# Two rounded token halves on ScalarE, the exact ones on VectorE, and the norm ahead in VectorE's queue

## The chip, the cores and the metric

The kernel runs on one core of a Trainium2 chip. The time is that of one execution on the device, in microseconds. The core's engines are TensorE (PE in the rows: matrix products and transposes; PEld is its weight load), VectorE (DVE), ScalarE (ACT), GpSimd (POOL) and SyncE (SP, which here only issues loads). They run side by side, each through its own queue, in the queue's order, and wait for each other through semaphores.

## The reference

Two layers of a decoder trunk on one sequence of 256 tokens with 1024 features, all in float32. Cut to what matters here:

```python
for l in range(2):
    mod = silu(c) @ w_ada[l] + b_ada[l]
    sh_m, sc_m, gt_m, sh_f, sc_f, gt_f = split(mod, 6)
    h = rms_norm(x, g_pre_mix[l]) * (1 + sc_m) + sh_m
    y = token_mixer(h, ...)                    # projection, two kinds of attention, output projection
    x = x + gt_m * rms_norm(y, g_post_mix[l])
    h = rms_norm(x, g_pre_ffn[l]) * (1 + sc_f) + sh_f
    y = conv_glu_ffn(h, ...)                   # (gelu(conv(h @ w_up_act)) * (h @ w_up_lin)) @ w_down
    x = x + gt_f * rms_norm(y, g_post_ffn[l])
```

The place of the change is the pair of lines between two sub-layers: the residual with its norm, and then the next sub-layer's norm and modulation.

## The kernel before

**Split numbers.** A product of full precision is made of three products of rounded numbers. Each operand is divided into a high part, rounded to the format fp32r (`hh` for tokens, `wh` or `dh` for weights), and a low part, the exact value less the high part (`hl`, `wl`, `dl`). `mm3` (L567 to L569) and `project` (L391) add high x high, low x high and high x low. A weight's split (`split`, L139 and L140) is a rounding copy on ScalarE and a subtraction on VectorE, each over 128x1024.

**Token tiles.** The 256 tokens are two tiles of 128. `xt` holds the running tokens with token rows on partitions. The products need the transposed form, with features on partitions: `hh` and `hl` have eight feature blocks of 128 (k = 0 to 7) by 256 tokens.

**A boundary.** `boundary` joins two sub-layers. There are three: mixer to FFN in layer 0, FFN of layer 0 to mixer of layer 1, and mixer to FFN in layer 1. Its inputs `ys` are four PSUM banks with the sub-layer's output, two halves of 512 features for each token tile. For each tile:

- `residual`: ScalarE squares each half with a running sum (L254), VectorE multiplies it by the gate row (L318, the gated product), GpSimd makes the factor one over the root (L262, L264), and VectorE adds the scaled product to `xt` (L326, two halves).
- `stat`: ScalarE squares the new tokens (L254), and GpSimd makes the second factor.
- `norm_T`: VectorE multiplies by this factor (L286, two halves), and TensorE transposes the halves, four 128x128 blocks (L274) into one PSUM bank each.
- `mod_T`: each block is multiplied by a column `scale` and gets a column `bias`. The rounded first half (k = 0 to 3) is written by ScalarE straight from the bank, block by block (L297). The second half is made exactly by VectorE (L300, four blocks, to an SBUF tile) and rounded by a copy on ScalarE (L305). The exact first half is made once more by ScalarE (L307, four blocks). At the end VectorE subtracts rounded from exact to get the low halves (L309, two of them).

**Order.** The program is traced in Python order; a compile-time scheduler then puts each engine's instructions into a queue, by the order of tracing and by when it reckons their inputs ready. `tc.issue_after(ins)` ties what is traced in its block, on the engine of `ins`, to a place behind `ins`. In a boundary the residual of tile 1 runs as a generator: its steps are taken between those of tile 0, and its last step (L326) is tied behind tile 0's last L300.

**After a boundary** to the FFN the first products are those of `lin`, 512 columns of `w_up_lin`, whose four weight units are loaded and split ahead, before the last rows of the output projection; the last unit (k = 6 and 7) takes its output buffer from the pool that the output projection's weights use. For each token tile `project` first runs all products with `hh`, and only then those with `hl` (`late="h"`). After the boundary to the mixer come the index projections `ia` and `ib`, with rotary embedding on VectorE (L357, L362), transposes (L368), index scores (L434) and the choice of the 64 best keys (L445, L446). Between them run products of the modulation on VectorE (L189).

Of the kernel before, what the change touches and what calls it, by code (L numbers as in the profile page):

```python
# [13 lines left out]
AF = mybir.ActivationFunctionType  # L14
OP = mybir.AluOpType
# [59 lines left out]
def trunk(ctx: ExitStack, tc, plan, x, c, stream, small, rope, out):  # L75
    nc = tc.nc
# [10 lines left out]
    def bank(i):  # L87
        return ps.tile([128, 512], F32, name=f"b{i}", tag=f"b{i}")
# [7 lines left out]
    def t2(dt=F32):  # L96
        return wrk.tile([128, 512], dt, name="t2", tag="t2", bufs=12)

    def big(name, dt=F32):
        return wrk.tile([128, 4, S], dt, name=name, tag="big", bufs=6)  # L100

    def tiny(n):
        return wrk.tile([128, n], F32, name=f"tiny{n}", tag=f"tiny{n}", bufs=8)


    st = {"off": 0, "behind": ()}

    def load(*units):

        n = sum(u[3] for u in units)  # L110
        t = wts.tile([128, 2048], F32, name="raw", tag="raw", bufs=6)
        nc.sync.dma_start(t[:, :n], bass.AP(tensor=stream.tensor, offset=stream.offset + st["off"],
                                            ap=[[n, 128], [1, n]]))
        st["off"] += 128 * n
        plan.append(units)
        r, o = [], 0
        for u in units:
            r.append(t[:, o:o + u[3]])
            o += u[3]
        return r  # L120

    def split(raw, where=None, pin=False, gain=None):
        n = raw.shape[-1]
        if where is None:
            hi = wts.tile([128, 1024], F32R, name="wh", tag="wh", bufs=5)
            lo = wts.tile([128, 1024], F32R, name="wl", tag="wl", bufs=5)
        else:
            hi = big("dh", F32R).rearrange("p a b -> p (a b)")
            lo = big("dl", F32R).rearrange("p a b -> p (a b)")
        with ExitStack() as behind:  # L130
            for ins in st["behind"]:
                behind.enter_context(tc.issue_after(ins))
            put = tc.keep_in_program_order if pin else lambda ins: ins
            if gain is not None:
                put(nc.scalar.activation(out=hi[:, :n], in_=raw, func=AF.Copy, scale=gain))
                put(nc.vector.scalar_tensor_tensor(out=lo[:, :n], in0=raw, scalar=gain, in1=hi[:, :n].bitcast(F32),
                                                   op0=OP.mult, op1=OP.subtract))
                return hi, lo
            put(nc.scalar.activation(out=hi[:, :n], in_=raw, func=AF.Copy))  # L139
            put(nc.vector.tensor_tensor(out=lo[:, :n], in0=raw, in1=hi[:, :n].bitcast(F32), op=OP.subtract))  # L140
        return hi, lo


    xt = con.tile([128, 2, D], F32, name="xt")
# [107 lines left out]
    def square(src, n, s, to=None):  # L252

        nc.scalar.activation(out=t2(BF) if to is None else to, in_=src, func=AF.Square, scale=float(n) ** -0.5, accum_out=s)  # L254

    def inv_root(s):

        r = tiny(1)
        if s.shape[-1] == 1:
            nc.gpsimd.tensor_scalar(out=r, in0=s, scalar1=EPS, scalar2=None, op0=OP.add)  # L260
        else:
            nc.gpsimd.tensor_scalar(out=r, in0=s[:, 0:1], scalar1=s[:, 1:2], scalar2=EPS, op0=OP.add, op1=OP.add)  # L262
        r2 = tiny(1)
        nc.gpsimd.tensor_tensor(out=r2, in0=r, in1=mhalf, op=OP.pow)  # L264
        return r2
# [5 lines left out]
    def turn4(x, b):  # L271
        p = bank(b)
        for j in range(4):
            nc.tensor.transpose(p[:, 128 * j:128 * j + 128], x[:, 128 * j:128 * j + 128], ident)  # L274
        return p

    def stat(t):
        s = tiny(2)
        for h in range(2):
            square(xt[:, t, 512 * h:512 * h + 512], D, s[:, h:h + 1])  # L280
        return inv_root(s)

    def norm_T(t, r, banks):
        xn = [t2(), t2()]
        for h in range(2):
            nc.vector.tensor_scalar(out=xn[h], in0=xt[:, t, 512 * h:512 * h + 512], scalar1=r, scalar2=None,  # L286
                                    op0=OP.mult)
        return [turn4(xn[h], banks[h]) for h in range(2)]

    def mod_T(p, t, scale, bias, hh, hl, between=None):  # L290

        part = lambda h, j: dict(scale=scale[:, 4 * h + j:4 * h + j + 1], bias=bias[:, 4 * h + j:4 * h + j + 1])
        quarter = lambda y, j: y[:, 128 * j:128 * j + 128]
        place = lambda y, h: y[:, 4 * h:4 * h + 4, 128 * t:128 * t + 128]
        f = t2(), t2()
        for j in range(4):
            nc.scalar.activation(out=place(hh, 0)[:, j], in_=quarter(p[0], j), func=AF.Identity, **part(0, j))  # L297
        for j in range(4):
            m = part(1, j)
            d = nc.vector.tensor_scalar(out=quarter(f[1], j), in0=quarter(p[1], j), scalar1=m["scale"],  # L300
                                        scalar2=m["bias"], op0=OP.mult, op1=OP.add)
        if between:
            between(d.ins)
        wide = [x.rearrange("p (k t) -> p k t", k=4) for x in f]
        nc.scalar.activation(out=place(hh, 1), in_=wide[1], func=AF.Copy)  # L305
        for j in range(4):
            a = nc.scalar.activation(out=quarter(f[0], j), in_=quarter(p[0], j), func=AF.Identity, **part(0, j))  # L307
        for h in (0, 1):
            d = nc.vector.tensor_tensor(out=place(hl, h), in0=wide[h], in1=place(hh, h).bitcast(F32), op=OP.subtract)  # L309
        return a.ins, d.ins  # L310

    def residual(t, y, g, to=None):

        s = tiny(2)
        d = [t2(), t2()]
        for h in range(2):
            square(y[h], D, s[:, h:h + 1])
            nc.vector.tensor_tensor(out=d[h], in0=y[h], in1=g[:, 512 * h:512 * h + 512], op=OP.mult)  # L318
            if h == 0:
                yield  # L320
        r = inv_root(s)
        yield
        parts = [(0, 512), (512, 256), (768, 256)] if to is not None and t else [(0, 512), (512, 512)]
        for i, (o, n) in enumerate(parts):
            xo = xt[:, t, o:o + n]
            nc.vector.scalar_tensor_tensor(out=xo, in0=d[o // 512][:, o % 512:o % 512 + n], scalar=r, in1=xo,  # L326
                                           op0=OP.mult, op1=OP.add)
            if to is not None:
                (nc.scalar if i % 2 else nc.sync).dma_start(to[:, o:o + n], xo)
        yield  # L330

    def boundary(ys, g, scale, bias, hh, hl):

        r0, r1 = residual(0, ys[0], g), residual(1, ys[1], g)
        for _ in range(3):
            next(r0)
        s0 = stat(0)
        next(r1)
        p0 = norm_T(0, s0, (4, 5))
        next(r1)  # L340

        def second(ins):
            with tc.issue_after(ins):
                next(r1)

        a = mod_T(p0, 0, scale, bias, hh, hl, second)
        s1 = stat(1)
        p1 = norm_T(1, s1, (6, 4))
        return a, mod_T(p1, 1, scale, bias, hh, hl)
# [23 lines left out]
    def project_units(l, name):  # L373
        n = len(CCOLS[name])
        per = 1024 // n
        u = [("b" if name == "lin" else "w", l, (name, k, min(per, 8 - k)), min(per, 8 - k) * n) for k in range(0, 8, per)]
        return [u[i:i + 2] for i in range(0, len(u), 2)]
# [383 lines left out]
    hh, hl, opened, first = start()  # L761

    for l in range(DEPTH):
# [90 lines left out]
        ys = [[bank(0), bank(1)], [bank(2), bank(3)]]  # L854
# [27 lines left out]
        while st["out"] < 2:  # L882
# [1 line left out]
        bg.run(out_first(range(3)))  # L884
        bg.drain("att", "out")
        out_load(4, 8)
        first = [[split(raw, "lin" if g < 1 or u < 1 else None) for u, raw in enumerate(load(*us))]
                 for g, us in enumerate(project_units(l, "lin"))]
        raws = []
        bg.run(out_last(range(3, 8)))  # L890
        bg.drain("sf")
# [2 lines left out]
        hh, hl = hT_tiles()  # L894
        scale, bias = pre_scale(l, "ffn")
        gate = gates["mix"]
        st["behind"] = boundary(ys, gate, scale, bias, hh, hl)[1]


        w0, w1, w2, bc = (scol(l, n) for n in ("w0", "w1", "w2", "bc"))  # L900
        ys = [[bank(0), bank(1)], [bank(2), bank(3)]]
        pend = []
        lin = [wrk.tile([128, 512], F32, name="lin", tag="o", bufs=3).rearrange("p (j t) -> p j t", j=2)
               for _ in range(2)]
# [68 lines left out]
        gate = gates["ffn"]  # L973
        bg.run(down(pend, (0, 1)))
        tps["free"] = [6, 7]
        if l + 1 < DEPTH:
            hh, hl = hT_tiles()
            scale, bias = pre_scale(l + 1, "mix")
# [85 lines left out]
```

## Time and profile before

| what | value |
|---|---|
| median of 3 runs | 690.02 us (689.62 to 690.02) |
| profiled execution | 689.88 us |
| its span in the trace | 688.1 us |
| TensorE busy | 664.8 us, 97% |
| VectorE busy | 547.6 us, 80% |
| ScalarE busy | 424.8 us, 62% |
| GpSimd busy | 26.2 us, 4% |

The span is what the profiler records of one execution; the 1.78 us between it and the execution's own time lie around it. A busy TensorE is not one at its peak, since products are pipelined. Times in the rows are microseconds from the start of the span; the granted clock of TensorE is at its full level in all stretches that the rows show.

### The profile page before, as it was taken

To read this page: it belongs to the slowest core of one execution; us is meant where nothing else is said; L and a number is where in the kernel's file an instruction comes from. 1 tells how busy PE (TensorE), PEld (TensorE's weight loads), DVE (VectorE), ACT (ScalarE), POOL (GpSimd) and SP (SyncE) were. 2 spreads that over 40 slices of the span, in tenths; PEclk is the share of its full clock that TensorE was granted. 3 is DMA by queue.
4 is the path that set the end of the run, shared out by engine and by line. 5 is a ranking of instruction groups with operands and counts; after the bars stand their busy time and mean duration, and the time that the engine had idled before them with its cause. 6 is when DMAs were issued, how large, how long until landed. Compare 5 with 4: busy or idle time off the path is not lost.

```text
span 688.1 us, 11317 instructions
## 1 busy us (share of the span) xinstructions
PE 664.8 (97%) x4329; PEld 569.6 (83%) x4329; DVE 547.6 (80%) x1085; ACT 424.8 (62%) x787; POOL 26.2 (4%) x56
## 2 busy tenths in 40 slices
PE   7999898999999999999999999999999999999996
PEld 4887676777999999999988677777789999999994
DVE  5878999878899999897679985677689886666553
ACT  5556687886955555555576558878696555555441
POOL 1000000002000000000020000000200000000001
PEclk9999999999999999999999999999999999999999
DMA  8999558963499998987436642346246885655001
GB/s 362 419 415 372 181 203 332 370 219 123 183 332 379 379 361 340 340 328 281 168 140 245 275 133 114 123 168 220 103 172 232 320 316 183 217 184 184 1 1 61
DMA packets 24518, 163.04 MB, mean 237 GB/s; under 512 B 3312, under 2 KB 3728, under 8 KB 6160
## 3 DMA queue, kind: packets, MB, share of 16 engines
q1 hardware_dynamic: 23184, 159.77, 61.8%
q0 software_dynamic: 704, 2.11, 1.0%
q8 instruction: 34, 0.56, 0.3%
q10 hardware_dynamic: 576, 0.43, 0.2%
q14 instruction: 20, 0.16, 0.1%
HBM read 161.24 MB, written 1.06 MB: 236 GB/s over the span
## 4 chain that ended last, share of the span: by engine, by line
PE 76%; DVE 12%; ACT 6%; issue 3%; POOL 1%; DMA 1%; SPq 0%; POOLq 0%; DVEq 0%; ACTq 0%
PE b L569 18%; PE b L567 18%; PE b L568 18%; PE b L391 12%; PE b L726 3%; DVE wl L140 3%; PE b L411 2%; DVE iscore L434 2%; ACT t L479 1%; DVE iscore L446 1%; ACT t L254 1%; DVE tiny L445 1%; PE b L494 1%; DVE raw L684 1%; DMA raw<-in_stream_dram 1%
## 5 line engine op out<-in xcount | busy, mean ns | idle before, releaser
L140 DVE TENSOR_TENSOR wl<-raw,wh 128x1024 fp32r<-128x1024 f32 (+1 forms) x146 | 172.8, 1195 | 36.9 <-ACT wh L139 31.3
L567 PE MATMUL b<-hh,wh 128*128 128x256 f32 x640 | 179.9, 281 | 0.0
L569 PE MATMUL b<-hl,wh 128*128 128x256 f32 x640 | 179.6, 281 | 0.0
L568 PE MATMUL b<-hh,wl 128*128 128x256 f32 x640 | 179.6, 281 | 0.0
L139 ACT ACTIVATE wh<-raw 128x1024 fp32r<-128x1024 f32 (+1 forms) x146 | 149.0, 1047 | 41.9 <-PE b L569 37.0
L568 PEld LDWEIGHTS b<-hh,wl 128*128 128x128 f32 x640 | 122.5, 191 | 1.3
L567 PEld LDWEIGHTS b<-hh,wh 128*128 128x128 f32 x640 | 120.2, 188 | 1.5
L569 PEld LDWEIGHTS b<-hl,wh 128*128 128x128 f32 x640 | 120.1, 188 | 0.0
L189 DVE SCALAR_TENSOR_TENSOR raw<-raw,crow 128x1024 f32<-128x1024 f32 x72 | 86.6, 1218 | 1.9 <-DMA raw<-in_stream_dram 1.9
L391 PE MATMUL b<-wh,hh 128*128 128x512 f32 (+1 forms) x184 | 73.0, 399 | 0.1
L391 PE MATMUL b<-wh,hl 128*128 128x512 f32 (+1 forms) x184 | 68.5, 387 | 0.0
L140 DVE TENSOR_TENSOR dl<-raw,dh 128x1024 fp32r<-128x1024 f32 (+2 forms) x47 | 56.8, 1211 | 13.2 <-ACT dh L139 12.4
L139 ACT ACTIVATE dh<-raw 128x1024 fp32r<-128x1024 f32 (+2 forms) x47 | 49.6, 1060 | 25.6 <-PE b L568 25.6
L944 ACT ACTIVATE t<-b,smt 128x256 f32<-128x256 f32 x44 | 25.1, 571 | 57.9 <-PE b L569 57.9
L567 PE MATMUL b<-dh,t 128*128 128x512 f32 x152 | 59.7, 393 | 0.0
L568 PE MATMUL b<-dh,t 128*128 128x512 f32 x152 | 59.6, 392 | 0.0
L569 PE MATMUL b<-dl,t 128*128 128x512 f32 x152 | 59.2, 389 | 0.0
L391 PE MATMUL b<-wl,hh 128*128 128x512 f32 (+1 forms) x184 | 55.6, 392 | 1.0 <-DVE wl L140 1.0
L391 PEld LDWEIGHTS b<-wh,hh 128*128 128x128 f32 x184 | 34.7, 189 | 8.7 <-issue 1.7
L391 PEld LDWEIGHTS b<-wl,hh 128*128 128x128 f32 x184 | 33.8, 189 | 7.2 <-DVE wl L140 1.4
L391 PEld LDWEIGHTS b<-wh,hl 128*128 128x128 f32 x184 | 33.8, 188 | 6.2 <-issue 0.6
L945 DVE SCALAR_TENSOR_TENSOR t<-b,smt,t 128x255 f32<-128x255 f32 x44 | 21.1, 480 | 20.6 <-ACT t L944 20.4
(172 smaller groups left out, 1098.5 us busy)
## 6 DMA issues: line engine op xcount, KB each, us to landing
raw<-in_stream_dram SPq DMA_DIRECT2D x143, 1024.0 KB, 5.9
raw<-in_stream_dram SPq DMA_DIRECT2D x8, 804.0 KB, 9.6
gate<-gated POOLq DMA_DIRECT2D x4, 512.0 KB, 6.5
xt<-in_x_dram SPq DMA_DIRECT2D x2, 512.0 KB, 4.3
raw<-in_stream_dram SPq DMA_DIRECT2D x1, 984.0 KB, 5.1
out_dram<-xt SPq DMA_DIRECT2D x2, 256.0 KB, 2.1
raw<-in_stream_dram SPq DMA_DIRECT2D x1, 328.0 KB, 4.2
out_dram<-xt ACTq DMA_DIRECT2D x1, 256.0 KB, 2.1
```

Of the source, the lines that this page charges most:

```text
L139: put(nc.scalar.activation(out=hi[:, :n], in_=raw, func=AF.Copy))
L140: put(nc.vector.tensor_tensor(out=lo[:, :n], in0=raw, in1=hi[:, :n].bitcast(F32), op=OP.subtract))
L189: nc.vector.scalar_tensor_tensor(out=ri, in0=ri, scalar=1.0, in1=crow, op0=OP.mult, op1=OP.mult, accum_out=mods[l][:, j + i:j + i + 1])
L391: mm = lambda l_, k, i, start=False, stop=False: nc.tensor.matmul(a[:, :n], lhsT=l_[:, k, tt], rhs=w[k][i], start=start, stop=stop)
L411: ins = nc.tensor.matmul(out, lhsT=lhsT, rhs=rhs, **flags)
L434: nc.vector.scalar_tensor_tensor(out=sc, in0=r[:, j * nk:j * nk + nk], scalar=wi[:, h:h + 1], in1=fill[:, 256 - nk:] if first else sc, op0 ...
L567: nc.tensor.matmul(y, lhsT=hh, rhs=wh, start=first, stop=False)
L568: nc.tensor.matmul(y, lhsT=hl, rhs=wh, start=False, stop=False)
L569: nc.tensor.matmul(y, lhsT=hh, rhs=wl, start=False, stop=last)
L726: pin(nc.tensor.matmul(acc[n, t], lhsT=y[:, k, 128 * t:128 * t + 128], rhs=w[k, u][part][:, c:c + m],  start=k == 0 and y is hh and part = ...
L944: nc.scalar.activation(out=z, in_=p[:, :256], func=AF.Identity, scale=w2[:, i:i + 1], bias=bc[:, i:i + 1])
L945: nc.vector.scalar_tensor_tensor(out=z[:, 1:], in0=p[:, :255], scalar=w1[:, i:i + 1], in1=z[:, 1:], op0=OP.mult, op1=OP.add)
```

## The change

In `mod_T` VectorE now makes both exact halves from the PSUM banks, the second half first, and ScalarE makes both rounded halves block by block from the same banks; the rounding copy from SBUF and ScalarE's exact quarters go. In `boundary` the norm of tile 0 is traced ahead of the first step of tile 1's residual (a square and a gated product). In the two boundaries to the FFN, the split of the last `lin` unit is traced behind that norm, with its VectorE half tied behind the norm's second instruction. The number of loads and of products stays.

```diff
     def norm_T(t, r, banks):
...
-            nc.vector.tensor_scalar(out=xn[h], in0=xt[:, t, 512 * h:512 * h + 512], scalar1=r, scalar2=None,
-                                    op0=OP.mult)
-        return [turn4(xn[h], banks[h]) for h in range(2)]
+            d = nc.vector.tensor_scalar(out=xn[h], in0=xt[:, t, 512 * h:512 * h + 512], scalar1=r, scalar2=None,
+                                        op0=OP.mult)
+        return [turn4(xn[h], banks[h]) for h in range(2)] + [d.ins]
...
         for j in range(4):
             nc.scalar.activation(out=place(hh, 0)[:, j], in_=quarter(p[0], j), func=AF.Identity, **part(0, j))
+        for h in (1, 0):
+            for j in range(4):
+                m = part(h, j)
+                d = nc.vector.tensor_scalar(out=quarter(f[h], j), in0=quarter(p[h], j), scalar1=m["scale"],
+                                            scalar2=m["bias"], op0=OP.mult, op1=OP.add)
+            if h and between:
+                between(d.ins)
         for j in range(4):
-            m = part(1, j)
-            d = nc.vector.tensor_scalar(out=quarter(f[1], j), in0=quarter(p[1], j), scalar1=m["scale"],
-                                        scalar2=m["bias"], op0=OP.mult, op1=OP.add)
-        if between:
-            between(d.ins)
+            a = nc.scalar.activation(out=place(hh, 1)[:, j], in_=quarter(p[1], j), func=AF.Identity, **part(1, j))
         wide = [x.rearrange("p (k t) -> p k t", k=4) for x in f]
-        nc.scalar.activation(out=place(hh, 1), in_=wide[1], func=AF.Copy)
-        for j in range(4):
-            a = nc.scalar.activation(out=quarter(f[0], j), in_=quarter(p[0], j), func=AF.Identity, **part(0, j))
...
-    def boundary(ys, g, scale, bias, hh, hl):
+    def boundary(ys, g, scale, bias, hh, hl, extra=None):
...
         s0 = stat(0)
+        p0 = norm_T(0, s0, (4, 5))
+        if extra:
+            extra(p0[-1])
         next(r1)
-        p0 = norm_T(0, s0, (4, 5))
         next(r1)
...
-        first = [[split(raw, "lin" if g < 1 or u < 1 else None) for u, raw in enumerate(load(*us))]
-                 for g, us in enumerate(project_units(l, "lin"))]
+        first = [load(*us) for us in project_units(l, "lin")]
+        first[0] = [split(raw, "lin") for raw in first[0]]
+        first[1][0] = split(first[1][0], "lin")
+
+        def last_split(ins):
+
+            st["behind"] = (ins,)
+            first[1][1] = split(first[1][1])
+            st["behind"] = ()
+
...
-        st["behind"] = boundary(ys, gate, scale, bias, hh, hl)[1]
+        st["behind"] = boundary(ys, gate, scale, bias, hh, hl, last_split)[1]
```

## Rows read from the trace of the kernel before

**Rows 1.** The page, busy us of each engine (share of the span) x instructions

```profile
PE 664.8 (97%) x4329; PEld 569.6 (83%) x4329; DVE 547.6 (80%) x1085; ACT 424.8 (62%) x787; POOL 26.2 (4%) x56
```

**Rows 2.** Windows: from:to and length, busy us (x instructions) by engine

```profile
core 0: us, PE busy (x) PEld busy (x) DVE busy (x) ACT busy (x) POOL busy (x), PEclk, DMA share, GB/s
162.00:172.00 10.00, 8.63 (x43) 6.43 (x43) 7.77 (x18) 7.10 (x21) 1.72 (x4) 1.00 0.46 179
351.00:361.00 10.00, 9.03 (x63) 8.11 (x62) 9.06 (x18) 8.85 (x23) 1.75 (x4) 1.00 0.56 212
492.00:502.00 10.00, 9.06 (x45) 6.67 (x44) 7.58 (x17) 7.22 (x21) 1.72 (x4) 1.00 0.29 106
```

**Rows 3.** Timeline of TensorE, first boundary: start, us, what, [idle before, releaser]

```profile
162.58 1.09 PE L274 MATMUL b<-ident,t 128*128 128x128 f32 x8 [0.43 <-DVE t L286]
163.78 0.50 PE L391 MATMUL b<-dh,hh 128*128 128x512 f32 x1
...
166.40 0.50 PE L391 MATMUL b<-dh,hh 128*128 128x512 f32 x1 [0.49 <-ACT hh L305]
...
168.36 0.84 PE L391 MATMUL b<-dh,hl 128*128 128x512 f32 x3
169.54 1.11 PE L274 MATMUL b<-ident,t 128*128 128x128 f32 x8 [0.34 <-DVE t L286]
...
171.65 0.39 PE L391 MATMUL b<-dh,hh 128*128 128x512 f32 x1
```

**Rows 4.** Timeline of VectorE, first boundary

```profile
160.30 1.23 DVE L140 TENSOR_TENSOR wl<-raw,wh 128x1024 fp32r<-128x1024 f32 x1 [0.60 <-ACT wh L139]
...
162.05 0.88 DVE L286 TENSOR_SCALAR t<-xt,tiny 128x512 f32<-128x512 f32 x2
...
163.71 1.37 DVE L300 TENSOR_SCALAR t<-b,prescale,mod 128x128 f32<-128x128 f32 x4
164.99 1.41 DVE L326 SCALAR_TENSOR_TENSOR xt<-t,tiny,xt 128x512 f32<-128x512 f32 x2
166.73 1.29 DVE L309 TENSOR_TENSOR hl<-t,hh 128x512 fp32r<-128x512 f32 x2 [0.33 <-ACT t L307]
169.00 0.88 DVE L286 TENSOR_SCALAR t<-xt,tiny 128x512 f32<-128x512 f32 x2 [0.97 <-POOL tiny L264]
```

**Rows 5.** Timeline of ScalarE, first boundary

```profile
163.28 1.51 ACT L297 ACTIVATE hh<-b,mod,prescale 128x128 fp32r<-128x128 f32 x4 [0.40 <-PE b L274]
...
166.56 0.66 ACT L254 ACTIVATE t<-xt 128x512 bf16<-128x512 f32 x1
```

**Rows 6.** Timeline of GpSimd, first boundary

```profile
159.95 0.56 POOL L264 TENSOR_TENSOR tiny<-tiny,mhalf 128x1 f32<-128x1 f32 x1
...
168.40 0.56 POOL L264 TENSOR_TENSOR tiny<-tiny,mhalf 128x1 f32<-128x1 f32 x1
```

**Rows 7.** Waits of VectorE in the whole span: total us, times, longest

```profile
DVE t L318 <- ACT t L254: 15.1, 10, 2.7
```

**Rows 8.** Timelines of VectorE and of GpSimd, second boundary

```profile
349.36 0.69 DVE L318 TENSOR_TENSOR t<-b,gate 128x512 f32<-128x512 f32 x1 [1.37 <-ACT t L254]
...
354.48 1.41 DVE L326 SCALAR_TENSOR_TENSOR xt<-t,tiny,xt 128x512 f32<-128x512 f32 x2
...
358.03 0.88 DVE L286 TENSOR_SCALAR t<-xt,tiny 128x512 f32<-128x512 f32 x2 [0.94 <-POOL tiny L264]
...
349.23 0.56 POOL L264 TENSOR_TENSOR tiny<-tiny,mhalf 128x1 f32<-128x1 f32 x1
```

**Rows 9.** Timeline of VectorE, third boundary

```profile
495.07 1.40 DVE L326 SCALAR_TENSOR_TENSOR xt<-t,tiny,xt 128x512 f32<-128x512 f32 x2
...
498.77 0.88 DVE L286 TENSOR_SCALAR t<-xt,tiny 128x512 f32<-128x512 f32 x2 [0.97 <-POOL tiny L264]
```

**Rows 10.** Windows behind the second boundary, columns as in rows 2

```profile
358.10:378.60 20.50, 20.03 (x126) 17.78 (x127) 20.50 (x44) 13.79 (x30) 1.16 (x2) 1.00 0.60 216
378.60:379.70 1.10, 1.10 (x7) 0.89 (x6) 0.43 (x4) 1.10 (x3) 0.00 (x0) 1.00 1.00 283
```

**Rows 11.** Timeline of TensorE at the choice of keys, layer 1

```profile
402.12 0.63 PE L368 MATMUL b<-ident,t 128*128 128x128 f32 x4 [0.65 <-DVE t L362]
```

## The prediction

> **What bounds the kernel now.** I read the busy times first. TensorE is busy for 97% of the span [rows 1], so time can only be won where it waits. Next I read the three stretches in which one sub-layer ends and the next begins, called here the first, second and third boundary (from 162, 351 and 492 us). In each, TensorE leaves 0.9 to 1.4 us of 10 unused [rows 2]: 1.37 + 0.97 + 0.94 = 3.3 us in all, which is 0.5% of the time. That is about all that a change inside these stretches can give, and 0.2% (1.38 us) is about what a measurement of this kernel can tell from no change.
>
> Then I read the timelines of the first boundary, engine by engine. TensorE stands still at three places [rows 3]. The transposes of token tile 0 wait 0.43 us for the norm (L286). The fifth pair of products waits 0.49 us for the second half of the rounded tokens (L305). The transposes of tile 1 wait 0.34 us for the second norm. VectorE has waits of its own here, 0.33 us before the low halves (L309) and 0.97 us before the second norm [rows 4]. These two are the only room that it has for more work. They add up to 1.30 us.
>
> **The change, part by part.**
>
> *Norm first (first and third boundary).* The factor of tile 0 is ready on GpSimd at 159.95 + 0.56 = 160.51 [rows 6], but VectorE takes a weight split at 160.30, then the gated product of tile 1, and the norm only at 162.05 [rows 4]. After the change the norm starts at 160.55, and TensorE has its input before the output projection ends at about 162.15 (162.58 less the idle 0.43). The wait of 0.43 us goes. This does not make VectorE free earlier: split, norm and two gated products still have to run before the modulation (L300). Before, they and a short wait filled 160.30 to 163.71, 3.41 us [rows 4]. Started at 160.55 they end by 163.96 at the latest; without that wait they end near 163.76. I take 163.8, which is 0.1 later than before. The split's ScalarE half keeps its place, since its output buffer is freed by the projection in both versions, and its result is needed only for the last quarter of the first products, so its delay of about 1.2 us is hidden by the products before them.
>
> *Rounded tokens by quarters on ScalarE.* The copy of the second half (L305) goes, and four quarters, one per 0.35 us (1.51 us for four [rows 5]), take the place of the four quarters that made the exact first half (L307). ScalarE has the copy less to do per tile.
>
> The trace says what the new quarters wait for. VectorE's gated product (L318) needs nothing that ScalarE's square of the same bank (L254) makes, and yet it waited for that square ten times, 15.1 us in all [rows 7]. So two engines' reads of one bank follow each other in traced order, and the new quarters of the second half come behind all four of VectorE's quarters. The Trainium skill has this as a rule ("PSUM — Partial Sum Buffer", section on bank collisions): two engines may not touch one bank at once, reads included. The trace agrees, with the ten waits named. Without that order the quarters could start behind the first four, at 163.28 + 1.38 = 164.66, and the products would not stop at all; with it they start at 163.8 + 1.37 = 165.2.
>
> With 165.2, the first quarter reaches TensorE about 0.5 us later (as 163.28 led to 163.78 [rows 3, 5]), at 165.7 instead of 166.40. So TensorE comes 0.7 us earlier to the point where it wants the low halves: 167.66 instead of 168.36 [rows 3].
>
> *Exact first half on VectorE.* This is the term that eats the gain. Four quarters more per tile cost VectorE 1.3 us (L300 starts at 163.71 and L326 at 164.99 [rows 4]), twice per boundary. The residual of tile 1 (L326) is queued directly behind the second half's quarters, so the new quarters come behind it. From 163.8: L326 at 165.1, new quarters at 166.5 (L326 holds 1.41), low halves at 167.8, first one done at about 168.5, both at 169.1, then the second norm at 169.1. Before, low halves began at 166.73 and the norm at 169.00. TensorE, ready at 167.66, now waits for the low halves until 168.5; it came there at 168.36. The squares of tile 1 start at 165.2 + 1.38 = 166.6, as before (166.56 [rows 5]), so the second factor still comes at 168.40 + 0.56 [rows 6]. In short, VectorE's 1.30 us of room is filled with 1.3 us of work, and what TensorE won earlier it waits out here.
>
> *First boundary, sum.* From the first low-half product at 168.36 to the next tile's products at 171.65 TensorE has 3.29 us, 0.34 of them idle [rows 3], so 2.95 of work. Started at 168.5 it can end at 171.45: 0.2 us won. If the queue still puts three products ahead of the transposes, these wait for the norm as before and 0.1 is lost. I take -0.2, ends -0.4 and +0.1. In tile 1 nothing waited, and 1.3 us more on VectorE fit ahead of its first FFN split.
>
> *Second boundary.* No split is moved, and TensorE had work until its transposes anyway. VectorE: L326 at 354.48, so new quarters at 355.89, low halves at 357.19, both done at 358.48; the second norm began at 358.03 [rows 8]. It is 0.45 us later, and 0.9 if the first norm is also queued ahead of the gated product of tile 1: that began at 349.36, and the norm's factor came only at 349.23 + 0.56 = 349.79 [rows 8], so VectorE would stand idle for 0.43 first. TensorE can fill a little with the other projection: +0.3. What follows weighs more. From 358.1 to 378.6 VectorE is busy 20.50 of 20.50 us, and in the 1.10 us after it has 0.67 free [rows 10]. Behind that come the index scores and the choice of keys, in which TensorE waits for VectorE's rotary results, 0.65 us at 402.12 [rows 11]. The second boundary puts 0.45 + 1.3 = 1.75 us into this full stretch (1.3 for tile 1, with no idle time to take it); 0.67 is absorbed, and 1.1 reaches this wait. It can be less: the modulation products (L189) in this stretch are wanted only at the end of the mixer, and the compile-time order may let one of them, 1.2 us, slip behind. Ends for the second boundary: 0 and +1.5 (0.9 + 1.3 - 0.67). I take +0.9, nearer the upper one, since the stretch is full.
>
> *Third boundary.* L326 at 495.07, new quarters 496.48, low halves 497.78 to 499.07; the second norm began at 498.77 [rows 9]. It is 0.3 late; TensorE can use part of that for low-half products that it had left behind the transposes. I take +0.05, ends -0.2 and +0.3. The DMA queues see no new transfer; the buffer of the moved split comes free some 1.2 us later, which counts only if a load is late, and no wait for a load stands on TensorE here.
>
> *Sum.* -0.2 + 0.9 + 0.05 = +0.75 us; the lower ends give -0.6, the upper ends +1.9. The profiled execution took 689.88 us (span 688.10 and 1.78 around it), so 690.63. The median of the runs, 690.02, lies 0.14 above that execution, so I say 690.8.
>
> **Rivals.**
>
> *VectorE takes the new quarters in its waits (faster).* Its two waits of the first boundary equal the new work in length, 1.30 us. If the order put two of the new quarters into each, the low halves would not be late, and what the earlier rounded tokens win would stay: 0.7 + 0.2 from the second transposes in the first boundary, about 0.3 in the second, 0.5 in the third, with nothing carried on behind the second: -1.7 us, 688.3. Against it: the first wait, 0.33, holds one quarter, and the queue is in order. If the reads of one bank did not wait for each other, as above, 0.5 more per boundary would be open, but the low halves would hold TensorE all the same.
>
> *The full stretch carries it all (slower).* The place is VectorE from 349 to 402 us. The price: the first norm queued ahead of the ready product (0.9 in place of 0.45), 1.3 for tile 1, only 0.67 absorbed: +1.5 there, and +0.4 if the other two boundaries keep their old order on TensorE. That makes +1.9, 691.9. It decides once more than 1.4 us reaches the wait at 402.12. For it speaks the row with 20.50 of 20.50; against it that L189 can slip.
>
> *The change doesn't act where it is meant to.* In the second boundary the gated product is ready before the factor [rows 8] and can stay ahead; the quarters just change places between two engines. Then only the first boundary's 0.43 moves, and that is given back before the low halves: 690.0.
>
> **How the numbers follow.** The forecast, some tenths up to one us slower, has 0.52; no effect 0.12; the faster rival 0.13; the slower one 0.23. Only the last two go past 1.38 us, so faster 0.13, same 0.64, slower 0.23. The range from 688.9 to 692.1 holds the ends of the sum and both sides up to where one in ten is left out on each.
>
> **What would show it.** After the change, I expect in the first boundary transposes with no wait for L286, the second half's first quarter on ScalarE right behind VectorE's fourth, a new TensorE wait of 0.5 to 0.9 us for the low halves, and second transposes at about the old place. Behind the second boundary VectorE should stay full past 378.6, with the wait at 402 moved by about 1 us. The prediction is wrong if VectorE takes the new quarters before L326 or between the low halves without delay, if tile 1's norm comes earlier than before, or if the order of index scores and key choice changes on VectorE, which the trace of before can't show.

## The result, and the profile after

The changed kernel takes 698.34 us (median of 4 runs, 698.28 to 698.71) against 689.89 us before (4 runs). The ratio is 1.0119, 95% interval 1.0107 to 1.0132: 8.45 us, or 1.2%, slower, where +0.8 us was forecast and 692.1 was the upper end of the range. The profiled execution took 698.71 us with a span of 696.9 us.

The windows of the three boundaries after, at the places that answer to [rows 2] (the later two have moved by 4 and 6 us), and four short windows behind the first boundary's low halves. Columns as in [rows 2]; PEclk is the granted clock as a share of 2.4 GHz:

```profile
162.00:172.00 10.00, 7.78 (x37) 5.58 (x36) 8.14 (x19) 6.02 (x18) 2.53 (x4) 0.94 0.46 176
355.00:365.00 10.00, 7.86 (x54) 6.80 (x53) 9.15 (x19) 7.80 (x18) 3.04 (x4) 1.00 0.57 211
498.00:508.00 10.00, 7.92 (x40) 5.63 (x38) 8.36 (x20) 5.97 (x18) 2.52 (x4) 1.00 0.30 106
168.00:170.00 2.00, 0.74 (x2) 0.30 (x2) 1.16 (x4) 0.00 (x0) 1.43 (x2) 1.00 0.00 0
170.00:172.00 2.00, 1.91 (x10) 1.78 (x11) 0.98 (x4) 1.21 (x4) 0.00 (x0) 0.71 0.03 8
172.00:174.00 2.00, 2.00 (x6) 1.55 (x5) 2.00 (x7) 0.30 (x1) 0.00 (x0) 0.50 0.00 0
174.00:176.00 2.00, 2.00 (x9) 1.59 (x9) 0.78 (x2) 1.93 (x6) 0.00 (x0) 0.94 0.00 0
```

TensorE leaves 2.1 to 2.2 us of ten unused in each boundary, where it left 0.9 to 1.4 [rows 2]; GpSimd, column five, is busy 2.5 to 3.0 us instead of 1.7. And between 170 and 176 the clock is not at full speed all the time: in one window it is 0.50, the lower of the two levels (1.2 GHz).

TensorE's timeline in the first boundary after (answers to [rows 3]):

```profile
161.87 1.03 PE L274 MATMUL b<-ident,t 128*128 128x128 f32 x8
...
165.46 0.50 PE L393 MATMUL b<-dh,hh 128*128 128x512 f32 x1 [0.20 <-ACT hh L306]
...
168.76 0.74 PE L393 MATMUL b<-dh,hl 128*128 128x512 f32 x2 [1.18 <-DVE hl L309]
170.09 1.32 PE L274 MATMUL b<-ident,t 128*128 128x128 f32 x8 [0.59 <-DVE t L286]
171.06 2.06 PE L393 MATMUL b<-dh,hl 128*128 128x512 f32 x4
172.92 1.05 PE L393 MATMUL b<-wh,hl 128*128 128x512 f32 x2
173.77 0.61 PE L393 MATMUL b<-dh,hh 128*128 128x512 f32 x1
```

The first transposes no longer wait, and the rounded quarters (now L306) hold TensorE for 0.20 us in place of 0.49 (a wait of 0.25 us for the first of L297, at 163.16, is new). Then 1.18 us are lost to the low halves and 0.59 to the second norm. The next tile's products begin at 173.77; before, 171.65 [rows 3]. In the third boundary the same four groups stand behind the same two waits, but at full clock:

```profile
504.81 0.73 PE L393 MATMUL b<-dh,hl 128*128 128x512 f32 x2 [1.18 <-DVE hl L309]
506.15 1.09 PE L274 MATMUL b<-ident,t 128*128 128x128 f32 x8 [0.60 <-DVE t L286]
507.00 1.17 PE L393 MATMUL b<-dh,hl 128*128 128x512 f32 x4
508.01 0.63 PE L393 MATMUL b<-wh,hl 128*128 128x512 f32 x2
```

The four products took 1.17 us here and 2.06 in the first boundary.

VectorE and, below it, GpSimd in the first boundary after (answer to [rows 4] and [rows 6]):

```profile
160.42 0.88 DVE L286 TENSOR_SCALAR t<-xt,tiny 128x512 f32<-128x512 f32 x2 [0.83 <-POOL tiny L264]
...
163.55 1.36 DVE L301 TENSOR_SCALAR t<-b,prescale,mod 128x128 f32<-128x128 f32 x4
164.82 1.41 DVE L326 SCALAR_TENSOR_TENSOR xt<-t,tiny,xt 128x512 f32<-128x512 f32 x2
166.15 1.36 DVE L301 TENSOR_SCALAR t<-b,prescale,mod 128x128 f32<-128x128 f32 x4
167.42 1.28 DVE L309 TENSOR_TENSOR hl<-t,hh 128x512 fp32r<-128x512 f32 x2
169.55 0.89 DVE L286 TENSOR_SCALAR t<-xt,tiny 128x512 f32<-128x512 f32 x2 [0.84 <-POOL tiny L264]
171.45 2.64 DVE L301 TENSOR_SCALAR t<-b,prescale,mod 128x128 f32<-128x128 f32 x8 [1.02 <-PE b L274]
...
176.10 0.69 DVE L309 TENSOR_TENSOR hl<-t,hh 128x512 fp32r<-128x512 f32 x1 [1.28 <-ACT hh L306]
177.05 1.23 DVE L140 TENSOR_TENSOR wl<-raw,wh 128x1024 fp32r<-128x1024 f32 x1 [0.26 <-ACT wh L139]
```

```profile
167.77 1.11 POOL L262 TENSOR_SCALAR tiny<-tiny 128x1 f32<-128x1 f32 x1 [3.98 <-ACT t L254]
168.96 0.56 POOL L264 TENSOR_TENSOR tiny<-tiny,mhalf 128x1 f32<-128x1 f32 x1
```

VectorE's queue ran in the order of the forecast, 0.2 to 0.4 us ahead of it, up to 168.70. GpSimd's addition of one column, L262, took 1.11 us; its mean over the kernel before was 0.32. So the second factor came at 169.52, and the second norm at 169.55 instead of 169.00 [rows 4].

ScalarE in tile 1 of the same boundary:

```profile
174.07 0.60 ACT L926 ACTIVATE t<-b 128x512 f32<-128x512 f32 x1 [1.77 <-PE b L393]
174.56 1.50 ACT L306 ACTIVATE hh<-b,mod,prescale 128x128 fp32r<-128x128 f32 x4
```

L926 copies tile 0's projection result. It stands ahead of tile 1's rounded quarters (L306) in ScalarE's queue, and it waits 1.77 us for TensorE. The quarters wait behind it; VectorE's four quarters of the same bank, the first half of the row at 171.45, were done by about 172.8. VectorE waits 1.28 us for them, and the first FFN split (L140) comes at 177.05; before it came at 175.12. Most of this wait goes with the low clock, at which tile 0's products end late. In the third boundary, at full clock, the copy stands at the same place and waits 0.38 us:

```profile
508.74 0.60 ACT L926 ACTIVATE t<-b 128x512 f32<-128x512 f32 x1 [0.38 <-PE b L393]
```

TensorE's longest waits by cause over the whole span (us, times, longest):

```profile
PE b L393 <- DVE hl L309: 3.3, 3, 1.2
PE b L569 <- DVE t L957: 2.9, 2, 1.6
PE b L370 <- DVE t L364: 2.7, 3, 1.0
```

The first two causes were not among the waits of before. L957 is a convolution step at the start of each FFN, where TensorE waits 1.3 us in layer 0 and 1.6 in layer 1. The third is the wait at the choice of keys [rows 11]: before, 1.1 us in two places, and 1.2 us in one place more that is put down to a split on ScalarE (L139), so 2.7 us stand against 2.3.

A ledger by stages, worked out from start times in each trace, says where the time went. S1 runs from the last square of the first boundary to the first FFN product, S2 from there to the second boundary's last square, S3 on to the third boundary's, S4 to the next FFN's first product, S5 to the final square. Before, they took 15.43, 174.11, 140.74, 14.92 and 174.21 us. Differences to these, for all kernels of this study that it helps to read:

| kernel | S1 | S2 | S3 | S4 | S5 |
|---|---|---|---|---|---|
| after | +2.50 | +1.57 | +1.86 | +1.23 | +1.81 |
| mod_only | +0.94 | +1.75 | +1.57 | +1.24 | +1.83 |
| order_only | -0.50 | +0.01 | +0.38 | +0.02 | +0.02 |
| exact_on_act | +0.29 | -0.02 | +1.52 | +0.81 | -0.08 |
| copy_behind | +0.90 | -0.04 | +1.74 | +1.23 | 0.00 |
| warm | +0.87 | +1.82 | +1.31 | +1.23 | +1.80 |
| copy_warm | +0.94 | -0.10 | +1.45 | +1.23 | +0.01 |
| ffn_alone | +0.87 | -0.01 | -0.02 | +1.27 | -0.08 |

The loss is in all five stages, and 3.4 us of it lie in the two FFN stages, in which the change edits nothing.

### The profile page after: what moved, and what is told of

Same layout as the page of the kernel before. It is cut to its first block, busy times and chain, and to the rows that moved or that the text cites. A ratio compares the mean times of both kernels' runs of the same rounds, so it can differ in the third digit from the quotient of the medians.

```text
span 696.9 us, 11342 instructions
## 1 busy us (share of the span) xinstructions
PE 667.2 (96%) x4329; PEld 571.0 (82%) x4329; DVE 555.1 (80%) x1109; ACT 422.4 (61%) x781; POOL 29.1 (4%) x56
## 4 chain that ended last, share of the span: by engine, by line
PE 72%; DVE 14%; ACT 7%; issue 4%; POOL 2%; DMA 1%; SPq 0%; POOLq 0%; DVEq 0%; ACTq 0%
PE b L569 17%; PE b L571 17%; PE b L570 17%; PE b L393 11%; DVE wl L140 3%; PE b L728 3%; PE b L413 3%; DVE iscore L436 2%; ACT t L481 1%; ACT t L254 1%; DVE iscore L448 1%; DVE tiny L447 1%; DVE dl L140 1%; PE b L496 1%; DVE raw L686 1%
## 5 line engine op out<-in xcount | busy, mean ns | idle before, releaser
L140 DVE TENSOR_TENSOR wl<-raw,wh 128x1024 fp32r<-128x1024 f32 (+1 forms) x146 | 173.2, 1197 | 33.4 <-ACT wh L139 28.8
L139 ACT ACTIVATE wh<-raw 128x1024 fp32r<-128x1024 f32 (+1 forms) x146 | 148.7, 1042 | 50.0 <-PE b L571 39.4
L140 DVE TENSOR_TENSOR dl<-raw,dh 128x1024 fp32r<-128x1024 f32 (+2 forms) x47 | 57.0, 1213 | 15.0 <-ACT dh L139 14.2
L139 ACT ACTIVATE dh<-raw 128x1024 fp32r<-128x1024 f32 (+2 forms) x47 | 49.5, 1055 | 23.4 <-PE b L570 23.4
```

## The experiments

**mod_only**: the new modulation with the old order of norm and split (only the second hunk of the diff).

> The changed modulation alone, with norm, split and gated product in their old order. Theory A (the exact quarters moved to VectorE cost the time: low halves late, second factor late, and late weight splits behind them): all of the loss stays, 698 to 699 us, some 0.4 more than the whole change, since the wait for the first norm comes back. Theory B (the new order of norm, split and gated product costs it): within 1 us of 690.

Measured: 696.92 us (696.49 to 699.62), ratio 1.0106 (1.0088 to 1.0125), 1.1 us below theory A's range and far from theory B's. Of the loss, 6.9 us come with the modulation alone. The 0.4 us that theory A expected on top did not come: S1 is +0.94, and +0.87 in warm, which has the new order and a full clock too. The rows also show that the fall of the clock needs more than the waits: with the same two waits, 1.18 and 0.60, the four products took 1.17 us.

```profile
168.81 0.73 PE L391 MATMUL b<-dh,hl 128*128 128x512 f32 x2 [1.18 <-DVE hl L309]
170.15 1.09 PE L274 MATMUL b<-ident,t 128*128 128x128 f32 x8 [0.60 <-DVE t L286]
170.99 1.17 PE L391 MATMUL b<-dh,hl 128*128 128x512 f32 x4
```

**order_only**: the new order, the old modulation (all hunks but the second).

> The new order alone, with the old modulation. Theory A: 689.2 to 690, since the wait of 0.43 us for the norm in the first boundary goes and nothing is put in its place; TensorE should show no wait for low halves. Theory B: the loss is here, 694 us or more.

Measured: 689.79 us, 0.9995 (0.9986 to 1.0005): no difference. The ledger shows why: 0.50 us won in S1 and 0.38 lost in S3, where VectorE stands idle for a factor with a ready product behind it.

**exact_on_act**: after, but the exact first half stays on ScalarE, traced behind the rounded quarters (in its queue three of the four exact quarters stand ahead of them).

```diff
-        for h in (1, 0):
             for j in range(4):
...
         for j in range(4):
             a = nc.scalar.activation(out=place(hh, 1)[:, j], in_=quarter(p[1], j), func=AF.Identity, **part(1, j))
+        for j in range(4):
+            a = nc.scalar.activation(out=quarter(f[0], j), in_=quarter(p[0], j), func=AF.Identity, **part(0, j))
```

> The whole change, but the exact first half stays on ScalarE, behind the rounded quarters; VectorE makes the exact second half alone, as before. Theory A: with the four quarters off VectorE the low halves come in time and the loss goes, 688.5 to 690. Theory C (not VectorE's work but the rounded quarters that wait for VectorE's reads of the same bank cost the time): the loss stays for the most part, 694 us or more.

Measured: 692.57 us, 1.0036 (1.0023 to 1.0050), between the two theories. 5.8 of the 8.45 us go with the engine that computes the exact first half, but this is not the price of VectorE's quarters alone. The compile-time order also put the copy of tile 0's result behind the quarters here, S2 and S5 are back at zero, and the clock stayed at 1.00 in the first boundary. And S3 keeps its loss, +1.52, though VectorE makes no quarters more than before.

**copy_behind**: after, with that copy tied behind tile 1's rounded quarters.

```diff
             r = t2()
-            nc.scalar.activation(out=r, in_=a, func=AF.Copy)
+            with tc.issue_after(st["behind"][0]):
+                nc.scalar.activation(out=r, in_=a, func=AF.Copy)
```

> The whole change, with ScalarE's copy of the first finished lin product tied behind the last rounded quarter of tile 1. In the changed kernel that copy stands ahead of these quarters in ScalarE's queue and waits for TensorE, and the FFN's first weight splits stand behind them. Theory D (this inverted order on ScalarE makes the splits late, and so the waits of 1.3 and 1.6 us for the convolution at the start of each FFN): those waits go, 695 to 696 us. Rival E (VectorE simply has too much to do there): the waits stay, 698 us.

Measured: 695.64 us (694.63 to 696.41), 1.0079 (1.0065 to 1.0093). TensorE's waits for L957 are gone, S2 and S5 are at zero; the waits for the low halves are 3.3 us, as in after. The gain of 2.7 us is less than the ledger's 3.4. The clock is the likely reason: in the profiled run, the fastest, it fell at the very start, a stretch that the change doesn't touch and where after had 1.00, and all that follows is 1.0 us late; two of the other runs have a lower mean clock still (0.993 against 0.996).

```profile
10.00:20.00 10.00, 8.77 (x42) 6.89 (x41) 8.28 (x17) 7.70 (x13) 0.00 (x0) 0.83 1.02 424
```

**warm**: after, with five products whose result nobody reads, in the wait for the low halves.

```diff
+            if name == "lin" and t == 0:
+                keep_warm(5)
             for k in range(8 if last else 0):
```

> The kernel after, with five TensorE products more whose result nobody reads, issued in the two FFN boundaries between tile 0's passes with the high halves and those with the low halves, where TensorE waits 1.18 us for VectorE in the kernel after. Theory: the fall of the granted clock in the first boundary (0.50 in its lowest 2 us) is a cost of its own, and 3.68 us from the second transposes to the third boundary's equivalent point against 2.33 us shows 1.35 us of it; with the wait filled the clock stays at 1.00 there and the time is about 697.0 us. Rival: the fall costs nothing that the waits do not cost already, and the time stays at 698.3 us, or rises by the fillers' own time (five of about 0.2 us, within the wait of 1.18 us).

Measured: 697.01 us (696.90 to 697.31), 1.0100 (1.0086 to 1.0114), as the theory had it. The second transposes stand at 170.18 (170.09 in after), so nothing came earlier; but what follows them runs at full clock:

```profile
170.00:172.00 2.00, 1.82 (x12) 1.68 (x13) 1.21 (x5) 1.12 (x4) 0.00 (x0) 1.00 0.00 0
172.00:174.00 2.00, 2.00 (x10) 1.60 (x10) 1.97 (x8) 1.61 (x6) 0.00 (x0) 1.00 0.00 0
```

**sub_extra and psum_extra**: before, with one subtraction more on VectorE (128x512, result unused) behind tile 0's low halves, where it idled 0.97 us. In the first both inputs come from SBUF, in the second one comes from PSUM.

```diff
         a = mod_T(p0, 0, scale, bias, hh, hl, second)
+        with tc.issue_after(a[1]):
+            nc.vector.tensor_tensor(out=t2(), in0=xt[:, 0, :512], in1=xt[:, 0, 512:], op=OP.subtract)
```

> The kernel before, with one VectorE subtraction of 128x512 more behind tile 0's low halves in the two FFN boundaries, both inputs from SBUF, its result unused; VectorE idles 0.97 us there before the second norm. Theory: GpSimd's 128x1 addition of the same moment cannot go on while a VectorE instruction with both inputs in SBUF runs, so it takes about 0.9 to 1.1 us in place of 0.30, and the second norm starts 0.5 to 0.7 us later than in the run with one input in PSUM. Rival: the addition is late in the kernel after for another reason (a queue, a semaphore), and stays at 0.30 us here.

> The same kernel as the one with the extra subtraction from SBUF, but one input of the extra subtraction is read from PSUM. Theory: GpSimd's addition stays at 0.30 us and the second norm starts when it did before (0.97 us idle less the subtraction's own time). Rival: any VectorE instruction there lengthens the addition as much as the one from SBUF does.

Measured: 691.01 and 691.09 us, 1.0014 (1.0005 to 1.0023) and 1.0015 (1.0006 to 1.0023). Their compile-time order differs from before's (all eight low-half products stand ahead of the second transposes), so they are read against each other. VectorE's extra subtraction, GpSimd's addition and the second norm, first with two inputs in SBUF:

```profile
167.95 0.69 DVE L349 TENSOR_TENSOR t<-xt 128x512 f32<-128x512 f32 x1
169.48 0.88 DVE L286 TENSOR_SCALAR t<-xt,tiny 128x512 f32<-128x512 f32 x2 [0.84 <-POOL tiny L264]
...
168.03 0.78 POOL L262 TENSOR_SCALAR tiny<-tiny 128x1 f32<-128x1 f32 x1 [4.09 <-ACT t L254]
```

and with one input in PSUM:

```profile
167.69 0.68 DVE L349 TENSOR_TENSOR t<-b,xt 128x512 f32<-128x512 f32 x1
168.74 0.88 DVE L286 TENSOR_SCALAR t<-xt,tiny 128x512 f32<-128x512 f32 x2 [0.37 <-POOL tiny L264]
...
167.77 0.30 POOL L262 TENSOR_SCALAR tiny<-tiny 128x1 f32<-128x1 f32 x1 [4.09 <-ACT t L254]
```

The addition takes 0.78 us beside the one and 0.30 beside the other, and ends in the first case 0.17 us after the subtraction. Counted from the last square (162.21 and 161.94), the norm stands at 7.27 and 6.80 us: 0.47 late. The Trainium skill has this rule ("SBUF — State Buffer", section "Who interferes with whom"): a VectorE instruction with two SBUF inputs contends with a GpSimd instruction that reads SBUF, and one of them waits for the other's end. The trace agrees, with 0.78 against 0.30. The times of the two kernels are equal, since TensorE still had low-half products to run here when the norm was late. So this pair shows the mechanism and not its price in after.

**order_ffn**: the new order in the two FFN boundaries alone, the old modulation everywhere.

> The new order alone (norm ahead of the eighth split) in the two FFN boundaries, none of the change in the second boundary, and the quarters computed where they were before. Theory: the order alone takes 0.5 us from the first boundary and nothing from the others; the second boundary loses 0.4 us by it, so leaving it out there gives about 689.4 us. Rival: no difference from the order in all three (689.8 us).

Measured: 689.35 us (689.10 to 690.31, 11 runs), 0.9990 (0.9981 to 0.9998). It is the fastest kernel of the study, by 0.1% (0.02 to 0.19%), which is below the 0.2% that was taken as the limit.

**copy_warm**: after with the edits of copy_behind and of warm.

> The kernel after with both earlier edits together: ScalarE's copy of the projection's result tied behind tile 1's rounded quarters, and the five unread products in TensorE's wait for the low halves. Theory that the two are separate costs: 698.34 less 2.70 and less 1.33 gives about 694.3 us. Rival: the copy's edit already took the fall of the clock away (its profiled execution shows a clock of 1.00 in the first boundary), so that the products add nothing and the time stays at 695.6 us.

Measured: 693.17 us (693.13 to 693.33), 1.0047 (1.0032 to 1.0062): even less than the sum. Against warm, where the clock is at 1.00 as well, tying the copy is worth 3.84 us, and S2 and S5 account for 3.71 of it. ScalarE's queue in tile 1 now:

```profile
172.49 1.51 ACT L306 ACTIVATE hh<-b,mod,prescale 128x128 fp32r<-128x128 f32 x4 [0.33 <-DVE t L301]
173.87 0.61 ACT L929 ACTIVATE t<-b 128x512 f32<-128x512 f32 x1
```

The quarters start at 172.49 instead of 174.56 (173.26 in warm), and the copy (here L929) waits for nothing. But that does not bring the first FFN split earlier: it comes 13.58 us behind the last square in warm (175.74) and 13.56 here (175.47). What differs between the two is VectorE's queue in the FFN. In warm a weight split stands between the two steps of the first convolution, and TensorE waits for the second:

```profile
183.98 0.48 DVE L957 SCALAR_TENSOR_TENSOR t<-b,smt,t 128x255 f32<-128x255 f32 x1
184.41 1.23 DVE L140 TENSOR_TENSOR wl<-raw,wh 128x1024 fp32r<-128x1024 f32 x1
185.55 0.47 DVE L959 SCALAR_TENSOR_TENSOR t<-b,smt,t 128x254 f32<-128x254 f32 x1
186.17 0.36 PE L571 MATMUL b<-hh,wh 128*128 128x256 f32 x1 [1.54 <-DVE t L959]
```

In copy_warm they follow each other, as they do before, and TensorE does not wait:

```profile
182.56 0.47 DVE L958 SCALAR_TENSOR_TENSOR t<-b,smt,t 128x255 f32<-128x255 f32 x1
183.07 0.48 DVE L960 SCALAR_TENSOR_TENSOR t<-b,smt,t 128x254 f32<-128x254 f32 x1
```

Seven splits stand ahead of the first step in warm, six in copy_warm and before.

**ffn_alone**: copy_warm with the second boundary as it was before, order and modulation.

> The kernel with both edits, and the second boundary as it was before: old order of the residual and the norm there, and the second half's quarters computed on VectorE, copied rounded by ScalarE, the first half's exact ones on ScalarE. Theory: the 1.9 us that the stretch from the second boundary to the third lost in the kernel after are lost inside the second boundary (from its last square to the first product of the next projection: 18.10 us after, 16.65 before), so the time falls by 1.5 to 1.9 us against the run with both edits alone. Rival: what is gained there is hidden by transfers or by the attention stage behind it, and the time falls by less than 0.5 us.

Measured: 691.86 us (691.69 to 691.98), 1.0028 (1.0017 to 1.0039): 1.31 us less, a little below the theory's range. S3 is at zero. What is left, 2.0 us, stands in S1 and S4, the two FFN boundaries themselves.

**low_psum**: copy_warm with tile 0's exact quarters in PSUM, to keep VectorE's subtractions off two SBUF inputs.

```diff
-        f = t2(), t2()
+        f = (t2(), t2()) if t else (p[0], bank(7))
```

> The kernel with both edits (693.17 us), with tile 0's exact quarters written to PSUM (the first half in its own bank, the second in a free one), so that VectorE's subtractions for the low halves have one input in PSUM and one in SBUF; same order of TensorE and VectorE. Theory: GpSimd's addition then takes 0.30 us in place of 1.11, the second norm starts about 0.5 us earlier and TensorE's wait for tile 1's transposes (0.60) nearly goes, in each boundary; the time falls by 0.5 us for each of the two FFN boundaries and at most as much for the second, to 691.7 to 692.2 us. Rival: the second norm is held by VectorE's own queue (the low halves end at 168.8, the norm can't start before) and the time stays at 693.2 us.

Measured: 698.40 us, 1.0126 (1.0109 to 1.0143): a miss. GpSimd's addition beside these quarters took 0.30 us, but four quarters into PSUM took 1.77 us in place of 1.36, the first half of the second norm went ahead of the low halves in the compile-time order, and in both FFNs the convolution kept TensorE waiting again (2.7 us): a split stands between its two steps here too, although the copy is tied. It changed too much at once, so it doesn't tell what GpSimd's 0.5 us cost in after.

## Why the prediction was wrong, step by step

The runs split the 8.5 us into four parts that add up, each the difference of two medians: the clock's fall 1.33 (after to warm), the compile-time order that comes with ScalarE's copy 3.84 (warm to copy_warm), the second boundary 1.31 (copy_warm to ffn_alone), and the two FFN boundaries 2.03 (ffn_alone to its own before, 689.83). The medians come from different sets of runs, in which before lies between 689.83 and 690.06, so each part is uncertain by some 0.2 us.

*Norm first*: right. The first transposes lost their wait, and the modulation began at 163.55 (163.8 forecast). The gain was real and worth 0.50 us in S1 (order_only), but nothing in S4, and the second boundary took 0.38 back through the very wait that the prediction named. Together with the new modulation even the 0.50 is not seen: S1 is +0.94 without the new order (mod_only) and +0.87 with it (warm).

*Rounded quarters behind VectorE's*: right. They started at 164.94, right behind VectorE's fourth quarter; 165.2 was forecast.

*"In tile 1 nothing waited, and 1.3 us more on VectorE fit ahead of its first FFN split"*: this step failed, and it cost most. VectorE's time was looked at, and the order behind it was taken to stay. It did not: the compile-time order put the copy of tile 0's result ahead of ScalarE's quarters, and in each FFN it put one weight split more ahead of the first convolution and one between its two steps on VectorE. TensorE then waited 1.3 to 1.6 us in each FFN, where the prediction had no term. Tying one copy brought the old order back, and with it 3.84 us. The four kernels with a split between the two steps (after, mod_only, warm, low_psum) have these waits; the other nine, before among them, have no such split and no such wait. That the splits came late is not the reason, as warm and copy_warm show. Why the compile-time order comes out as it does stays open.

*"So the second factor still comes at 168.40 + 0.56"*: failed. The squares ended in time, at 167.7, but the low halves had moved onto GpSimd's addition (1.11 us), and the factor was there at 169.52. The prediction asked what is queued behind VectorE's new work on VectorE, not what else runs in those microseconds.

*"Low halves at 167.8, first one done at about 168.5"*: failed in what TensorE waits for. The low halves began at 167.42, earlier than forecast, yet the products started at 168.76, 0.06 after both were done (168.70); in the third boundary it is the same. Why the first product waits for both is open. The wait is 1.18 us, where 0.5 to 0.9 was forecast, 3.3 us in all three boundaries.

These two steps make the first boundary's sum wrong: the next tile's products began 0.86 us later than before at full clock (172.51 in warm against 171.65), where -0.2 was forecast. In the third boundary, where +0.05 was forecast and the norm had no wait to lose, S4 is +1.23. S1 and S4 together are +2.1 us in ffn_alone. How much of that is GpSimd's 0.55 us twice, and how much the low halves, wasn't separated.

*The clock* was no term of the sum. Behind the new waits of the first boundary it fell to 0.50, and from the second transposes to the next tile's products TensorE took 3.68 us against 2.33 in the third boundary (506.15 to 508.48). Of this size is what warm gave back: 1.33 us by the medians, 1.63 in S1 of the profiled executions, since the clock was still low when the next tile began.

*Second boundary*: the number came near, by luck. +0.9 was forecast with +1.5 as the upper end, and 1.31 measured (1.45 in S3 of copy_warm). But the forecast had +0.3 from TensorE in the boundary itself, and the rest from up to 1.1 us that VectorE's full stretch was to carry on to the choice of keys. The first product of the next projection, the one with 512 columns, shows that it was the other way round. It comes 16.43 us behind the last square before (368.16 less 351.73) and 17.87 in copy_warm (370.16 less 352.29). The rows are before's and then copy_warm's:

```profile
368.16 0.39 PE L391 MATMUL b<-wh,hh 128*128 128x512 f32 x1
```

```profile
359.45 0.72 PE L393 MATMUL b<-dh,hl 128*128 128x328 f32 x3 [0.92 <-DVE hl L309]
370.16 0.39 PE L393 MATMUL b<-wh,hh 128*128 128x512 f32 x1
358.66:379.16 20.50, 19.10 (x118) 16.92 (x119) 19.36 (x45) 12.82 (x29) 2.07 (x3) 1.00 0.45 166
```

So 1.44 us are lost up to this product, where TensorE's wait of 0.92 us for the low halves is new, and behind it 0.0 in copy_warm (between -0.1 and +0.4 in after, copy_behind and warm, which have the same code there). The last row is the stretch that answers to [rows 10]: VectorE is busy 19.36 of 20.50 us in it, so it was not full any more. Which part of the edit costs the 1.44 us is open: exact_on_act, with no quarters more on VectorE, loses 1.64 us up to the same product.

The rivals: the slower one had the right sign, but its path, a full VectorE behind the second boundary, carried nothing on in copy_warm. The faster one fell: the low halves did hold TensorE. So did the one without effect.

## What to carry to other kernels

When work moves from one engine to another, the compile-time order of every queue behind it can change, also in stages that no edit touches: compare the order of the instructions there, not only their times. When a filled gap is counted as free, list the instructions of the other engines that ran in it. And a new wait on a busy TensorE can cost more than its own length; compare the length of the same products behind it.

## What the runs showed of the hardware

An addition of one column on GpSimd took 1.11 us beside VectorE subtractions with two SBUF inputs, and 0.78 beside a single one that was put there for the purpose; with one input in PSUM it stayed at 0.30.

TensorE's clock fell to its lower level (0.50 of 2.4 GHz) behind waits of 1.18 and 0.59 us in the first boundary of after's profiled execution. The mean clocks of its four runs (0.994 to 0.995, against 0.997 to 0.999 in warm) fit a fall in each of them, without showing where. It stayed at 1.00 behind equal waits in the third boundary, and in the first boundary of mod_only. What decides between these is open; with five unread products in the first wait (warm) it stayed at 1.00 in the first boundary.
